# Storing the low parts of the input projection's weights once and reloading them

## The chip, the cores and the metric

The kernel runs on one core of one Trainium2 chip. The metric is the device time of one execution in microseconds (us). Before the change it was 2847.2 us in the median of 3 runs (2840.0 to 2849.79).

## The reference

One layer over 1024 tokens of width 2048, in float32. The input is normalised (RMSNorm) and projected once to 5968 columns, `z = xn @ w_in`. A part of z feeds RWKV-7, a recurrence with a 64 x 64 state in each of 16 heads, token by token. Another feeds sparse attention: an indexer scores all keys for each query, the best 256 admissible keys are selected, and 16 heads attend to them. Both outputs are gated, concatenated and projected:

```
xn = rms_norm(h, norm_g); z = xn @ w_in
z_rw, g_rw, q_lat, kv_lat, k_idx, w_idx, g_ds = split(z)
o_rw = rwkv7_mixer(z_rw, ...); o_ds = dsa_mixer(q_lat, kv_lat, k_idx, w_idx, ...)
h = h + concat(o_rw * silu(g_rw), o_ds * silu(g_ds)) @ w_out
h = h + (p @ ple_w) * sigmoid(h @ ple_gate_w)
out = rms_norm(h, final_g)
```

## The kernel before

Large matrix products are computed in a fast reduced-precision format with correction: both operands are split into a high part (rounded to that format) and a low part (the rest), and three products are summed, high by high, high by low and low by high.

The tokens are handled in two halves of 512 (`hf` 0 and 1), one after the other. The activations of a half (`xh`, `xl`, 16 tiles of 128 channels each) stay on chip. The weights do not: for each half, each of 46 column tiles of `w_z` (128 columns) is streamed as 4 pieces of 128 x 512 numbers (256 KB), 184 pieces in all, and one narrower tile `w_z80` (80 columns) as 4 more. A piece is prepared in `w_piece` (lines 507 to 515): SyncE (SP) issues a load into a buffer `wr` (4 buffers), ScalarE (ACT) rounds it into `wh` (5 buffers), and GpSimd (POOL) subtracts, `wl = wr - wh` (5 buffers). TensorE (PE) then runs 12 matmuls of 128 x 512 on it in `gemm_part`: four channel tiles, three products each. So the same piece is loaded, rounded and subtracted once for each half.

In the same stretch the recurrence runs as 32 steps (`sub`): 8 units of two heads, in two halves, in two quarters of 256 tokens each. A step has a preparation, `chunk_setup`, a long dependent sequence over PE, VectorE (DVE), ACT and POOL (normalising keys, decays, the products `ARb`, `BRb`, `KB`, a triangular inverse by five doublings, `Qf`), and a serial part over 4 chunks of 64 tokens, `chunk_serial`, which runs beside the next step's preparation. A step needs the projections r, k, v and gate of its unit (`zunit`). Projections that no step waits for are the latents of the attention (`dsa_lat`), its gates (`gds`, eight tiles for each half), and the first part of the output projection (`wout_rw`).

The order on each engine is not the order of the program text. `Sched` records all instructions of a stage, a planner (`plan`) simulates the engines with prices and levels, and `emit` writes the instructions out in the planned order; each engine then executes its own list in that order. Chain instructions have level 0, the splitting of weights `LSPLIT` = 1, the projections' matmuls `LG` = 3, the rest `LF` = 4; a lower number goes first. PE takes the fills in short runs between the chain's matmuls. The planner counts a DVE instruction that uses two on-chip operands and a POOL instruction as excluding each other. SP issues every DMA, in its planned order.

When the last step is done the buffers of the recurrence are given up (`nc.emit(RP)`, line 1015), and the second stage begins in their room: index scores of all queries (level `LX` = 2), then the key selection, a bitwise search in which DVE and ACT count, with the rest of the output projection's first part as filler on PE. Attention, the rest of the output projection and the gated second projection follow; these use `w_piece` too, with other weights.

`kept` (lines 911 to 924) already does for the output projection's first part what the change does for the input projection: in the first half it stores `wh` and `wl` in DRAM, in the second it loads both.

Of the kernel before, what the change touches and what calls it, by code (L numbers as in the profile page):

```python
# [10 lines left out]
F32 = mybir.dt.float32  # L11
# [17 lines left out]
LB, LA, LC, LEVAC, LSPLIT, LX, LG, LF, LSQ = 0, 0, 1, 1, 1, 2, 3, 4, 4  # L29
# [356 lines left out]
def hybrid_kernel(ctx, tc, cst, msk, bkt, prm, xt, pt_, w_z, w_z80, w_lora, w_uq, w_iq, w_uk, w_uv, w_o, w_pg,  # L386
                  w_pl, rel_bias, out):
    ctx.enter_context(tc.manual_schedule())
    nc = Sched(tc.nc)
    dram = ctx.enter_context(tc.tile_pool(name="dram", bufs=1, space=DRAM))  # L390
    dt = lambda n, shape: dram.tile(shape, F32, name=n)
# [2 lines left out]
    kid = [dt(f"ki{h}", [64, TH]) for h in range(2)]  # L394
    gdd, h1d = ([[dt(f"{n}{j}_{h}", [128, TH]) for h in range(2)] for j in range(m)] for n, m in (("gd", 8), ("h1", 16)))
    bsk, vbd = dt("bsk", [16, 128, 384]), dt("vb", [16, 384])
    parts = {}

    def pool(stack, keep=None, **kw):
        p_ = Pool(nc, stack.enter_context(tc.tile_pool(**kw)), kw["bufs"])  # L400
# [106 lines left out]
    def w_piece(src, kn, n):  # L507
        wr = wp.tile([128, 4, 128], F32, name="wr", tag="wr", bufs=W_[0])
        nc.sync.dma_start(wr[:, :kn, :n], src.rearrange("p (k n) -> p k n", k=kn))
        with nc.level(LSPLIT):  # L510
            wh = wp.tile([128, 4, 128], F32R, name="wh", tag="wh", bufs=W_[1])
            nc.scalar.activation(wh[:, :kn, :n], wr[:, :kn, :n], AF.Copy)
            wl = wp.tile([128, 4, 128], F32R, name="wl", tag="wl", bufs=W_[1])
            nc.gpsimd.tensor_tensor(wl[:, :kn, :n], wr[:, :kn, :n], wh[:, :kn, :n], op=OP.subtract)
        return wh, wl

    def gemm_part(pz, src, n, k0, kn, nk, xh, xl, w=None):
        wh, wl = w or w_piece(src, kn, n)
        for k in range(kn):
            kk = k0 + k  # L520
            for j, (a, b) in enumerate(((wh, xh), (wh, xl), (wl, xh))):
                nc.tensor.matmul(pz[:n], a[:, k, :n], b(kk), start=(kk == 0 and j == 0),
                                 stop=(kk == nk - 1 and j == 2), skip_group_check=True)
# [16 lines left out]
    def zgroup(tiles, before=lambda g, piece: None):  # L540
        pzs = [pz_tile() for _ in tiles]
        for g in range(4):
            early = []
            before(g, lambda: early.append(w_piece(w_z[tiles[len(early)], g], 4, 128)))
            for j, (pz, i) in enumerate(zip(pzs, tiles)):
                gemm_part(pz, w_z[i, g], 128, g * 4, 4, 16, xh_, xl_, early[j] if early else None)
        return pzs
# [363 lines left out]
    def kept(n, g):  # L911

        if (n, g) in parts:
            pair = []
            for d, nm in zip(parts[n, g], ("wh", "wl")):
                t = wp.tile([128, 4, 128], F32R, name=nm, tag=nm, bufs=W_[1])
                nc.sync.dma_start(t.bitcast(F32), d)
                pair.append(t)
            return pair
        pair = w_piece(w_o[n, g], 4, 128)  # L920
        parts[n, g] = [dt(f"wo{n}_{g}{a}", [128, 4, 128]) for a in "hl"]
        for d, t in zip(parts[n, g], pair):
            nc.sync.dma_start(d, t.bitcast(F32))
        return pair
# [605 lines left out]
```

## Time and profile before

| | |
|---|---|
| time, median of 3 runs | 2847.2 us |
| the profiled execution's own time | 2844.57 us |
| its span, first to last instruction | 2842.8 us |
| mean granted TensorE clock | 0.976 |
| weight pieces split on POOL, all stages | 624 |

PE is the tensor engine's matmuls and PEld its weight loads; the ends of matmuls are modelled, and overlapping ones are counted once in busy times. Since every instruction is issued through one helper, all carry the line number 382; instructions are told apart by the names of the tiles that they write and read, as in `wl<-wr,wh`. Second half means hf = 1, which begins at about 745 us; the first stage with the recurrence ends at about 1600 us.

### The profile page before, as it was taken

What the parts mean: (1) busy time and instruction counts of PE and PEld (TensorE: products, weight loads), DVE (VectorE), ACT (ScalarE), POOL (GpSimd) and SP (SyncE); (2) the same over time, 40 slices, a digit from 0 to 9 for tenths busy, and PEclk for the clock granted to TensorE, in tenths of its full rate; (3) what the DMA queues carried; (4) which work ended last, traced back from release to release, by engine and by line L of the source; (5) the groups of instructions that cost most, each with busy time, mean ns of one, the idle gap of its engine ahead of it and who ended that gap; (6) DMA issues with size and microseconds to landing.
All of it is one profiled execution on the core that took longest, in us unless ns stands there. A gap on an engine that the chain in (4) does not pass through costs nothing. (4 is left out here: it accounts for less than half of the span.)

```text
span 2842.8 us, 46633 instructions
## 1 busy us (share of the span) xinstructions
PE 2701.8 (95%) x16482; PEld 2157.9 (76%) x16482; DVE 1644.8 (58%) x3709; ACT 1482.0 (52%) x3265; POOL 1336.5 (47%) x1371
## 2 busy tenths in 40 slices
PE   7999999999999999999999999948999999999996
PEld 5777778778778778777877788826776788878885
DVE  6457667546764566667665478987666641135312
ACT  5445555535654355555555466895767533343332
POOL 5545445555455545545555421023334455656654
PEclk9999999999999999999999999968999999999998
DMA  4232222232332222222227844511223343355332
GB/s 159 82 116 70 68 71 75 75 89 71 99 100 84 89 68 68 71 69 70 79 82 240 310 146 137 175 36 39 73 65 90 102 138 97 97 157 174 103 99 92
DMA packets 172586, 293.36 MB, mean 103 GB/s; under 512 B 23440, under 2 KB 44992, under 8 KB 172352
## 3 DMA queue, kind: packets, MB, share of 16 engines
q1 hardware_dynamic: 172352, 290.38, 32.9%
q8 instruction: 130, 2.13, 0.3%
q14 instruction: 104, 0.85, 0.1%
HBM read 232.87 MB, written 52.19 MB: 100 GB/s over the span
## 5 line engine op out<-in xcount | busy, mean ns | idle before, releaser
L382 POOL TENSOR_TENSOR wl<-wr,wh 128x512 fp32r<-128x512 f32 (+1 forms) x624 | 812.8, 1306 | 773.5 <-ACT wh L382 720.4
L382 ACT ACTIVATE wh<-wr 128x512 fp32r<-128x512 f32 (+1 forms) x624 | 384.1, 617 | 731.7 <-PE pz L382 536.1
L382 PE MATMUL pz<-xh,wh 128*128 128x512 f32 (+1 forms) x1504 | 609.5, 407 | 11.5 <-ACT wh L382 7.6
L382 PE MATMUL pz<-xh,wl 128*128 128x512 f32 (+1 forms) x1504 | 610.2, 408 | 2.3 <-POOL wl L382 2.1
L382 PE MATMUL pz<-xl,wh 128*128 128x512 f32 (+1 forms) x1504 | 611.1, 408 | 0.0
L382 PEld LDWEIGHTS pz<-xh,wh 128*128 128x128 f32 (+1 forms) x1504 | 285.6, 190 | 62.5 <-ACT wh L382 9.4
L382 PEld LDWEIGHTS pz<-xh,wl 128*128 128x128 f32 (+1 forms) x1504 | 285.1, 190 | 51.4 <-POOL wl L382 5.5
L382 PEld LDWEIGHTS pz<-xl,wh 128*128 128x128 f32 (+1 forms) x1504 | 285.8, 190 | 45.9 <-DVE xl L382 0.3
L382 DVE SCALAR_TENSOR_TENSOR tg<-tg,pg 128x512 f32<-128x512 f32 x32 | 22.0, 687 | 314.3 <-ACT tg L382 303.1
L382 DVE CAST_PREDICATED QX<-MS,pq 128x512 f16<-128x512 uint8 x160 | 110.3, 689 | 158.7 <-PE pq L382 157.6
L382 PE MATMUL pz<-hh,wh 128*128 128x512 f32 x512 | 199.3, 389 | 0.0
L382 PE MATMUL pz<-hh,wl 128*128 128x512 f32 x512 | 199.3, 389 | 0.0
L382 PE MATMUL pz<-hl,wh 128*128 128x512 f32 x512 | 199.2, 389 | 0.0
L382 POOL TENSOR_TENSOR mb<-mk,bt 128x256 f32<-128x256 f32 (+1 forms) x128 | 89.2, 702 | 153.6 <-DVE mx L382 126.3
L382 ACT ACTIVATE Ztb<-pzt 64x256 f16<-64x256 f32 x320 | 120.6, 377 | 61.3 <-PE pzt L382 55.9
L382 ACT ACTIVATE lgt<-lgt,nm 128x128 f32<-128x128 f32 (+7 forms) x128 | 98.8, 772 | 55.0 <-DVE nm L382 54.2
L382 PE MATMUL ptt<-C,lgt 128*128 128x128 f32 x576 | 99.7, 289 | 23.8 <-ACT lgt L382 22.4
L382 ACT ACTIVATE Sw<-UV,Wx 64x64 f32<-64x64 f32 x240 | 82.2, 342 | 58.9 <-DVE UV L382 55.5
L382 PEld LDWEIGHTS pz<-hh,wh 128*128 128x128 f32 x512 | 96.1, 188 | 20.0
L382 PEld LDWEIGHTS pz<-hl,wh 128*128 128x128 f32 x512 | 96.1, 188 | 20.0
L382 PEld LDWEIGHTS pz<-hh,wl 128*128 128x128 f32 x512 | 96.1, 188 | 19.7
L382 PE MATMUL po<-PT,V 128*64 128x128 f32 x1152 | 87.6, 287 | 18.7 <-ACT PT L382 18.2
(331 smaller groups left out, 6008.3 us busy)
## 6 DMA issues: line engine op xcount, KB each, us to landing
wr<-in_w_z_dram SPq DMA_DIRECT2D x368, 256.0 KB, 2.6
wr<-in_w_pg_dram SPq DMA_DIRECT2D x128, 256.0 KB, 2.6
wr<-in_w_o_dram SPq DMA_DIRECT2D x88, 256.0 KB, 2.9
h<-h SPq DMA_DIRECT2D x60, 256.0 KB, 3.2
h<-in_xt_dram SPq DMA_DIRECT2D x32, 256.0 KB, 3.7
out_dram<-h SPq DMA_DIRECT2D x32, 256.0 KB, 2.3
gd<-gd SPq DMA_DIRECT2D x16, 256.0 KB, 2.3
mix<-m SPq DMA_DIRECT2D x32, 128.0 KB, 1.7
```

Of the source, the lines that this page charges most:

```text
L382: getattr(self.real[o.eng], o.name)(*o.args, **o.kw)
```

## The change

The first time that a piece of `w_z` or `w_z80` is prepared, its low part is also stored in a new DRAM tile, at level `LF`. When the same piece is asked for again (found by tensor name and offset), the high part is made as before, from a new load of the weights, and the low part is loaded from DRAM in place of the subtraction, at the level of the splitting. Nothing else is edited; the planner makes new orders for all engines from the new list of instructions.

```diff
-    parts = {}
+    parts, lows, KEEP = {}, {}, (w_z.tensor.name, w_z80.tensor.name)
...
             wl = wp.tile([128, 4, 128], F32R, name="wl", tag="wl", bufs=W_[1])
+            key = src.tensor.name, src.offset
+            if key in lows:
+                nc.sync.dma_start(wl[:, :kn, :n].bitcast(F32), lows[key])
+                return wh, wl
             nc.gpsimd.tensor_tensor(wl[:, :kn, :n], wr[:, :kn, :n], wh[:, :kn, :n], op=OP.subtract)
+        if src.tensor.name in KEEP:
+            lows[key] = dt(f"low{len(lows)}", [128, kn, n])
+            with nc.level(LF):
+                nc.sync.dma_start(lows[key], wl[:, :kn, :n].bitcast(F32))
         return wh, wl
```

## Rows read from the trace of the kernel before

**Rows 1.** Page, busy time, share of the span and instructions of each engine

```profile
PE 2701.8 (95%) x16482; PEld 2157.9 (76%) x16482; DVE 1644.8 (58%) x3709; ACT 1482.0 (52%) x3265; POOL 1336.5 (47%) x1371
```

**Rows 2.** Chain of waits: start us, us, what; one of 15 such

```profile
2623.75 10.88 PE pz L382 x48
```

**Rows 3.** Busy time by stage: us, busy (instructions), PEclk, DMA share, GB/s

```profile
945.00:1390.00 445.00, 444.15 (x3118) 354.99 (x3117) 291.94 (x559) 234.55 (x610) 227.03 (x238) 1.00 0.24 70
...
1600.00:1780.00 180.00, 177.50 (x806) 145.74 (x805) 131.55 (x158) 107.42 (x158) 39.09 (x31) 0.99 0.52 178
1780.00:1850.00 70.00, 67.25 (x375) 58.50 (x374) 67.63 (x263) 59.93 (x108) 6.00 (x6) 1.00 0.54 174
1850.00:1930.00 80.00, 36.75 (x156) 23.99 (x155) 68.57 (x305) 73.92 (x146) 17.63 (x20) 0.62 0.11 29
```

**Rows 4.** Tile hr, 940 to 1530 us: count, ns min/median/max, first and last start

```profile
L382 POOL TENSOR_TENSOR hr<-hs,nh x15: 1001/1006/1318, 945.4 to 1523.6; 128x4 f32<-128x4 f32 x15
```

**Rows 5.** Tile wl, matmuls on PE, 945 to 1512 us

```profile
L382 PE MATMUL pz<-xh,wl x558: 387/393/586, 945.0 to 1511.6; 128*128 128x512 f32 x186
```

**Rows 6.** Tile gd on DVE, 900 to 1600 us

```profile
L382 DVE SCALAR_TENSOR_TENSOR gd<-gd,zd x8: 673/693/1553, 1401.3 to 1515.0; 128x512 f32<-128x512 f32 x8
```

**Rows 7.** Waits of PEld, 745 to 1512 us: total us, times, longest

```profile
PEld pz L382 <- POOL wl L382: 0.4, 2, 0.2
```

**Rows 8.** Groups on POOL, 945 to 1512 us: count, busy us, mean ns, idle before

```profile
L382 POOL TENSOR_TENSOR wl<-wr,wh 128x512 fp32r<-128x512 f32 x140 | 184.6, 1319 | 196.6 <-ACT wh L382 181.0 <-PE pz L382 5.0 <-PE pv L382 4.1
L382 POOL TENSOR_TENSOR BRb<-r,Wx 64x256 f32<-64x256 f32 x28 | 22.3, 796 | 4.4 <-ACT Wx L382 3.4
```

**Rows 9.** Groups on DVE, 945 to 1512 us

```profile
L382 DVE TENSOR_TENSOR ARb<-kkn,Wx 64x256 f32<-64x256 f32 x28 | 24.6, 878 | 1.6 <-ACT Wx L382 1.1
L382 DVE SCALAR_TENSOR_TENSOR KB<-q,iW 64x256 f32<-64x256 f32 x28 | 21.5, 768 | 0.3
L382 DVE TENSOR_TENSOR KB<-kp,iW 64x256 f32<-64x256 f32 x28 | 20.4, 730 | 0.2
...
L382 DVE TENSOR_TENSOR kp<-tha,k 128x256 f32<-128x256 f32 x14 | 11.7, 836 | 0.4
...
L382 DVE COPY hx<-hr 128x256 f32<-128x256 f32 x14 | 8.8, 626 | 2.2 <-POOL hr L382 2.2
```

**Rows 10.** Tiles on DVE, 945 to 1512 us: ns min/median/max, first and last

```profile
L382 DVE TENSOR_TENSOR ARb<-kkn,Wx x28: 417/823/1423, 949.3 to 1487.0; 64x256 f32<-64x256 f32 x28
...
L382 DVE SCALAR_TENSOR_TENSOR KB<-q,iW x28: 406/424/1519, 953.0 to 1488.7; 64x256 f32<-64x256 f32 x28
L382 DVE TENSOR_TENSOR KB<-kp,iW x28: 406/424/1521, 956.4 to 1491.2; 64x256 f32<-64x256 f32 x28
...
L382 DVE TENSOR_TENSOR kp<-tha,k x14: 424/427/1430, 953.9 to 1489.1; 128x256 f32<-128x256 f32 x14
...
L382 DVE COPY hx<-hr x14: 279/678/1371, 947.1 to 1481.5; 128x256 f32<-128x256 f32 x14
```

**Rows 11.** Timeline of POOL, DVE and PE in one step: start, us, instruction

```profile
1326.74 1.58 POOL L382 TENSOR_TENSOR wl<-wr,wh 128x512 fp32r<-128x512 f32 x1 [0.29 <-ACT wh L382]
1329.43 1.40 POOL L382 TENSOR_TENSOR wl<-wr,wh 128x512 fp32r<-128x512 f32 x1 [1.11 <-ACT wh L382]
1330.80 0.73 POOL L382 TENSOR_TENSOR rk<-r,kp 128x256 f32<-128x256 f32 x1
...
1328.84 0.84 DVE L382 TENSOR_TENSOR KB<-kp,iW 64x256 f32<-64x256 f32 x2
...
1332.79 1.05 PE L382 MATMUL pA<-ARb,KB 128*128 128x128 f32 x8
```

**Rows 12.** Busy time by stage, the second ten microseconds of the kernel

```profile
10.00:20.00 10.00, 10.00 (x38) 8.06 (x37) 10.00 (x9) 9.02 (x16) 7.35 (x11) 1.00 1.00 346
```

**Rows 13.** DMA issues: count, KB each, median us to landing

```profile
wr<-in_w_z_dram SPq DMA_DIRECT2D x368, 256.0 KB, 2.6
...
wl<-wo_0l SPq DMA_DIRECT2D x16, 256.0 KB, 3.7
```

## The prediction

> **What bounds the kernel now.** I read the page's busy times first. TensorE (PE) is busy 95% of the span, GpSimd (POOL) 47% [rows 1], so the obvious verdict is that relieving POOL is worth nothing. The chain of waits agrees at the end of the kernel: 48 matmuls take 10.88 us, one each 0.2267 us with nothing between them [rows 2]. A weight piece is 12 such matmuls, 2.72 us of PE.
>
> But a full PE is only a bound if nothing better could be put in its place, so I went on to the table by stage. From 945 to 1390 us PE is busy 444 of 445 us; from 1600 to 1930 us it is idle 2.5 + 2.75 + 43.25 = 48.5 us, most of it in the key selection (1850 to 1930 us), where VectorE (DVE) is busy 68.6 and ScalarE (ACT) 73.9 of 80 us and the granted clock falls to 0.62 [rows 3]. PE has filler (weight pieces and output tiles) in the first part, and has run out of it in the last. The key selection comes behind the index scores, and these can start only when the recurrent chain of `chunk_setup` has ended, because their buffers take the room of its pools. So what counts is when the chain ends. Filler displaced by a faster chain is not lost: it goes into those 48.5 us.
>
> Is the chain bound by latency or by PE? Its marker is the `hr` instruction, one in each of the 32 steps: the last 15 lie between 945.4 and 1523.6 us [rows 4], so 14 intervals of 41.3 us. From 945 to 1512 us PE makes 558 matmuls on low parts, that is 139.5 pieces [rows 5], 379 us at 2.72 us; the other 188 us are 13.7 steps of chain work, 13.7 us each. One head unit (two steps) must have 16 pieces and twice the chain work: 43.5 + 27.4 = 70.9 us, 35.5 us a step. The measured 41.3 us is 5.8 us above that floor. The surplus goes into projecting ahead: the eight `gds` tiles, the filler of lowest priority, are evacuated only from 1401 us on [rows 6], with `hr` still coming up to 1523.6 us [rows 4]. So latency sets the step.
>
> **The change, part by part.**
>
> *Removed: 184 subtractions on POOL in the second half.* PE hardly waits for them itself: in the second half the weight loads waited 0.4 us for `wl` in all [rows 7]. That term I put at nothing. The gain, if there is one, is in what these subtractions do to others. From 945 to 1512 us 140 of them take 184.6 us, 1.32 us each [rows 8], a third of POOL's time. DVE instructions of the chain that read two SBUF operands show two durations: `KB` 0.41 us at best and 0.42 in the median, but up to 1.52 us [rows 10]. I take each group's busy time [rows 9] less count times its shortest [rows 10]: `hx` 8.8 - 14 x 0.279 = 4.9, `ARb` 24.6 - 28 x 0.417 = 12.9, `KB` from q 21.5 - 11.4 = 10.1, `kp` 11.7 - 5.9 = 5.8, `KB` from kp 20.4 - 11.4 = 9.0; together 42.7 us in 14 steps. Who causes it? POOL's `BRb` (22.3 us, rows 8) lies in the same place and stays. If all of it is charged first, 20.4 us are left for `wl`; shared by POOL time, 184.6 / 206.9 of 42.7, it is 38 us. I take the middle, 29 us.
>
> The Trainium skill (SBUF — State Buffer, "Who interferes with whom") says that a DVE instruction with two SBUF inputs and a GpSimd instruction that reads SBUF exclude each other, and whichever issued first blocks the other fully. The trace agrees with the form of it: the excess of the longest `KB`, 1.1 us, is most of one subtraction. By that rule every one of the 42.7 us is somebody's lock, and with the pieces spread at random `wl` would have the 38 us rather than the 29: a sum 9 us better.
>
> *Removed with it: waiting in POOL's own queue.* In the step at 1326 us one subtraction starts at 1326.74, the next at 1329.43, and `rk` starts only behind it at 1330.80; PE has the product on `rk` ahead of `pA`, which starts at 1332.79, though the last `KB` was done at 1329.68 [rows 11]. POOL is in a subtraction a third of the time, so a POOL instruction of the chain finds one in its way with that chance and waits half of 1.32 us: 0.2 us. Four on the path (`hr`, `BRb`, `rk`, `IX`) in 14 steps make 12 us at most, 0 at least; I take 6.
>
> So the chain would end 29 + 6 = 35 us earlier (from 20 to 50). PE's order is written out in advance by the kernel's own planner, which counts POOL against DVE too; it will set fewer fillers between the chain's matmuls. Since the 48.5 us of idle PE behind it exceed 35 us, all of it reaches the end; what is late next is filler, beyond a gain of 48.5 us.
>
> *Added: 184 stores in the first half*, 256 KB each. They wait for `wl`, and SyncE (SP) queues behind them; but the next load of `wr` into that buffer already waits for the same subtraction. POOL waits for nothing new while the store takes less than the four pieces that PE still has ahead (10.9 us). Only the start is tight: from 10 to 20 us DMA is at 1.00 of its time, at 346 GB/s [rows 12]. Twelve stores there are 12 x 0.262 MB / 346 GB/s = 9.1 us if all delay a load, 0 if they fill the gaps. I take 3 us.
>
> The Trainium skill (SBUF — State Buffer, "SBUF: two separate sides") says that engine ports and DMA ports are disjoint, so that a DMA cannot be slowed by a compute instruction or the reverse; by it the 94 MB of extra traffic cost the engines nothing, and the sum loses only what the transfers take from each other. No row here tests that.
>
> *Added: 184 loads in the second half.* A piece now lands twice, `wr` in 2.6 us and the low part in about 3.7 us, which the existing reload of `wo` shows [rows 13]. With five buffers it may be issued four pieces (10.9 us) ahead. DMA's share from 945 to 1390 us is 0.24 [rows 3]; the pieces' first landing is nearly all of its 70 GB/s (140 x 0.262 MB in 567 us are 65), so the share would about double. Hidden, at 0; if the cover is gone PE waits for each piece (rival 3). ACT's conversion of the high part stays. SP's queue has the load where it had the wait for POOL.
>
> **Sum.** 2844.6 us of the profiled execution (span 2842.8) - 35 + 3 = 2812.6. The median of the runs shown, 2847.2, is 2.6 us above that execution, so I forecast **2815 us**. Its own ends: -50 + 0 gives 2797, -20 + 9 gives 2836.
>
> **Rivals.**
> 1. *The chain gains nothing* (chance 0.14). For it: PE shows 444 of 445 us busy, and its written order may be re-planned with as much filler between the chain's steps; DVE instructions that get shorter then only wait longer. Against it: 5.8 us a step above PE's floor. Removed waits 0.4 us, start +3: about 2850 us, within 0.3% (8.5 us, about what a measurement of this kernel can tell from no change) of before.
> 2. *The chain gains more than POOL's share*, because a looser plan also shortens its waits on PE (0.16). Down to the floor it would be 14 x 5.8 = 81 us, but idle PE behind it has only 48.5: 2799 us or a little less.
> 3. *Slower: the low parts land too late* (0.14). SP issues in order. If a load of a low part stands in its queue for a buffer that PE has not yet released, everything behind it, `wr` included, waits too. It decides where landing and queueing together exceed 10.9 us, so a queue wait beyond 7.2 us. The half switch and the latent tiles, where PE runs pieces back to back, are its place. At 0.1 us for each of 184 pieces and the 9 us of the start it is 2847 + 27 = 2874 us with no gain from the chain. Against it: DMA at 0.24.
>
> That the change doesn't do what it says (a key that never matches) would leave only the stores, and fall under rival 1.
>
> **Numbers.** Forecast 0.56, rivals 0.14, 0.16, 0.14. Faster by over 0.3%: 0.56 + 0.16 = 0.72; within: 0.14; slower: 0.14. Range 2795 to 2852: it holds the forecast, most of rival 1 and the upper part of rival 2, and leaves out most of rival 3.
>
> **What would show it.** In the table by stage of the changed kernel, POOL at about a fifth of the second half; the 14 intervals of `hr` at about 38.8 us; `KB` and `kp` nearer their shortest; the key selection ending some 32 us earlier, and PE's idle time there shorter by as much. Wrong: intervals still at 41 us (rival 1), weight loads waiting for the low parts' transfers (rival 3), or an index stage that starts earlier and then takes longer, so that the gain is given back.

## The result: 2799 us, and the profile after

The changed kernel took 2799.2 us (median of 4 runs, 2793.5 to 2801.9), the kernel before 2847.4 us beside it: a ratio of 0.9832, with a 95% interval of 0.9808 to 0.9857, so 48 us faster. The forecast was 2815 us; 2799 us is the number that stood for rival 2 (the chain gains more, down to PE's floor). It lies in the stated range, 2795 to 2852, near its lower end.

The page of the changed kernel, first the busy times (the same columns as [rows 1]), then the traffic and three of its DMA issues (as [rows 13]):

```profile
PE 2693.5 (96%) x16482; PEld 2150.1 (77%) x16482; DVE 1584.2 (57%) x3709; ACT 1489.8 (53%) x3265; POOL 1109.4 (40%) x1183
...
DMA packets 229805, 391.19 MB, mean 140 GB/s; under 512 B 33552, under 2 KB 55104, under 8 KB 229568
...
wr<-in_w_z_dram SPq DMA_DIRECT2D x368, 256.0 KB, 2.9
low<-wl SPq DMA_DIRECT2D x184, 256.0 KB, 3.2
wl<-low SPq DMA_DIRECT2D x184, 256.0 KB, 2.6
```

PE has the same 16482 instructions. POOL has 188 fewer and 227 us less work, and 184 stores and 184 loads of 256 KB are new, with four of 160 KB each way for the narrow tile: 97.8 MB more traffic than the 293.4 MB of before. The profiled span is 2799.8 us, 43.0 us shorter. Since PE is at work nearly all the time, the 43.0 us can be split by PE's own time: idle time went from 2842.8 - 2701.8 = 141.0 to 2799.8 - 2693.5 = 106.3 us, which is 34.7 us less, and the same matmuls took 8.3 us less.

The marker of the recurrent chain in the changed kernel answers to [rows 4]:

```profile
L382 POOL TENSOR_TENSOR hr<-hs,nh x15: 1007/1008/1377, 955.0 to 1456.1; 128x4 f32<-128x4 f32 x15
```

Fourteen intervals are 501.1 us, 35.8 us each; before they were 41.3. The first of the 15 starts 9.6 us later than before, the last 67.5 us earlier. The floor that the prediction worked out was 35.5 us.

Where the steps became shorter is seen in PE's matmuls on low parts, of which each weight piece has four. Between the first and the last of the 15 markers the kernel before has

```profile
L382 PE MATMUL pz<-xh,wl x559: 387/393/586, 945.0 to 1512.4; 128*128 128x512 f32 x187
```

and the changed kernel

```profile
L382 PE MATMUL pz<-xh,wl x451: 387/393/776, 956.1 to 1455.8; 128*128 128x512 f32 x151
```

That is 27 pieces less between the steps, 73 us of PE at 2.72 us each, of the 77 us by which the 14 intervals became shorter. What is left is 32.2 such matmuls a step; the prediction's floor, eight pieces a step, has 32.

The table by stage of the changed kernel, the same windows and columns as [rows 3]:

```profile
945.00:1390.00 445.00, 442.57 (x3256) 351.38 (x3255) 281.79 (x630) 251.19 (x659) 98.18 (x147) 1.00 0.40 126
1600.00:1780.00 180.00, 175.48 (x788) 143.07 (x787) 155.48 (x358) 131.41 (x213) 52.51 (x36) 1.00 0.69 232
1780.00:1850.00 70.00, 67.97 (x314) 55.34 (x313) 62.49 (x230) 60.73 (x108) 13.24 (x7) 1.00 0.71 232
1850.00:1930.00 80.00, 70.35 (x500) 56.45 (x499) 54.05 (x181) 48.82 (x100) 37.09 (x40) 0.94 0.21 58
```

PE is as full as before in the recurrence (442.6 of 445 us), but with more done: DVE and ACT issue 71 and 49 instructions more in it. Of 1600 to 1930 us PE is now idle 4.5 + 2.0 + 9.7 = 16.2 us where it was 48.5. That is 32.3 of the 34.7 us. Of the rest, PE is idle 7.0 us more in the first 750 us, 1.4 more from there to 1600 us, and 10.8 less after 1930 us. The granted clock of the last row went from 0.62 to 0.94.

What PE waited for from 1600 to 1950 us (total us, times, longest), first the kernel before:

```profile
PE ptt L382 <- ACT lgt L382: 21.8, 5, 12.5
PE plg L382 <- DVE mx L382: 21.3, 9, 5.5
```

and the changed kernel:

```profile
...
PE plg L382 <- DVE mx L382: 2.8, 4, 1.6
...
PE ptt L382 <- ACT lgt L382: 0.2, 1, 0.2
```

`plg` and `ptt` are the first matmuls of attention; their softmax (`mx` on DVE, `lgt` on ACT) had to stand behind the key selection on both engines. The selection's counting on ACT, from the kernel before:

```profile
L382 ACT ACTIVATE js<-mk,th x93: 920/1041/1153, 1786.4 to 1918.9; 128x1024 f16<-128x1024 f32 x31, 128x896 f16<-128x896 f32 x31, 128x768 f16<-128x768 f32 x31
```

and from the changed one:

```profile
L382 ACT ACTIVATE js<-mk,th x93: 921/1043/1152, 1714.5 to 1838.0; 128x1024 f16<-128x1024 f32 x31, 128x896 f16<-128x896 f32 x31, 128x768 f16<-128x768 f32 x31
```

It ends 81 us earlier. PE's filler, the first part of the output projection, no longer ends ahead of it but beside it. These are its matmuls in the changed kernel from 1780 to 1900 us:

```profile
L382 PE MATMUL pz<-ml,wh x81: 388/389/397, 1779.9 to 1835.6; 128*128 128x512 f32 x81
```

Before, the last one was at 1818.9 us. So the selection ends 81 us earlier, PE's idle time could take up less than that, and the kernel ends 43 us earlier in the profile. What is late now should be filler; this is tested below.

### The profile page after: what moved, and what is told of

Same layout as the page of the kernel before. It is cut to its first block, busy times and chain, and to the rows that moved or that the text cites. A ratio compares the mean times of both kernels' runs of the same rounds, so it can differ in the third digit from the quotient of the medians.

```text
span 2799.8 us, 47033 instructions
## 1 busy us (share of the span) xinstructions
PE 2693.5 (96%) x16482; PEld 2150.1 (77%) x16482; DVE 1584.2 (57%) x3709; ACT 1489.8 (53%) x3265; POOL 1109.4 (40%) x1183
## 5 line engine op out<-in xcount | busy, mean ns | idle before, releaser
L382 POOL TENSOR_TENSOR wl<-wr,wh 128x512 fp32r<-128x512 f32 (+2 forms) x436 | 574.6, 1321 | 561.0 <-ACT wh L382 528.7
L382 DVE SCALAR_TENSOR_TENSOR mk<-rl,WI,mk 128x384 f32<-128x384 f32 (+2 forms) x90 | 101.1, 1165 | 9.2 <-ACT rl L382 8.8
L382 PE MATMUL pz<-mh,wh 128*128 128x512 f32 x256 | 99.5, 393 | 5.5 <-DMA wh<-wo_0h 3.2
```

Of the source, the lines that this page charges most:

```text
L382: getattr(self.real[o.eng], o.name)(*o.args, **o.kw)
```

## The experiments

Those named together ran on the same chip. Each ratio is to the kernel before on that chip.

### Stores alone, and loads alone

`e1_stores_only` leaves the subtractions of the second half in place:

```diff
-            if key in lows:
-                nc.sync.dma_start(wl[:, :kn, :n].bitcast(F32), lows[key])
-                return wh, wl
-        if src.tensor.name in KEEP:
+        if src.tensor.name in KEEP and key not in lows:
```

> Stores of the first half alone; the second half subtracts as before the change. Theory (the stores cost the first half what the trace after shows, hr of step 17 at 955.0 instead of 945.4 us, and nothing else changes): about 2857 us, intervals of hr in the second half still 41 us. Rival (the stores cost nothing, the delay is only the planner's other order): 2845 to 2850 us.

Measured: 2855.2 us against 2847.2, ratio 1.0033 (1.0020 to 1.0046). The stores cost 8 us. Its `hr` intervals are 41.3 us, from 959.2 to 1537.8 us: the recurrence of the second half is untouched and starts 14 us late.

`e2_loads_only` stores one piece of each width and lets all 184 loads read that one, so that the low parts of the second half are those of another piece:

```diff
-                nc.sync.dma_start(wl[:, :kn, :n].bitcast(F32), lows[key])
+                nc.sync.dma_start(wl[:, :kn, :n].bitcast(F32), lows[n])
...
+            if n not in lows:
+                lows[n] = dt(f"low{n}", [128, kn, n])
+                with nc.level(LF):
+                    nc.sync.dma_start(lows[n], wl[:, :kn, :n].bitcast(F32))
```

> Loads of the second half alone: one piece of each width is stored, and all 184 loads read that one, so the low parts of the second half have the wrong numbers; the traffic of the loads is the same, 182 stores are left out. Theory (stores cost some 10 us of PE time in the first half, which reach the end): 2789 us, step 17 at 945 us, intervals of hr at 36 us. Rival (what bounds the end is something behind the chain, so an earlier chain gives nothing more): 2799 us.

Measured: 2792.6 us, ratio 0.9811 (0.9794 to 0.9828); `hr` from 945.4 to 1445.7 us, 35.7 us a step. The start of the 15 steps is that of before to the tenth, so the 9.6 us that the changed kernel loses there are the stores'. At the end of the kernel about 6 us of it are seen, within the width of the two intervals.

Where do the stores cost? In the first 750 us PE is idle 23.6 us before and 30.6 after. ACT's waits there for a fresh weight piece, in the kernel before (total us, times, longest):

```profile
ACT wh L382 <- DMA wr<-in_w_z_dram: 24.7, 11, 8.1
```

and in the changed kernel:

```profile
ACT wh L382 <- DMA wr<-in_w_z_dram: 43.0, 22, 6.9
```

The fresh weight piece comes late, twice as often. Over kernels with different stores (some of them are told further down) this wait and PE's idle time mostly go together:

| first 750 us | ACT's wait for `wr` | PE idle | DMA share |
|---|---|---|---|
| before | 24.7 | 23.6 | 0.29 |
| e2_loads_only (2 stores) | 25.4 | 25.3 | 0.29 |
| v4_units_early_store (112 stores) | 24.7 | 27.6 | 0.39 |
| e8_store_without_hold (172 stores) | 33.1 | 26.4 | 0.47 |
| v5_rkv_only (84 stores) | 37.0 | 27.8 | 0.38 |
| v1_units_only (112 stores) | 38.7 | 27.9 | 0.40 |
| e1_stores_only | 40.3 | 31.7 | 0.49 |
| the changed kernel | 43.0 | 30.6 | 0.49 |
| e3_old_order | 59.5 | 35.6 | 0.46 |

The last row has the longest wait without the highest DMA share, so traffic alone does not set it. `v4_units_early_store` has more idle time than before without a longer wait, so late weights are not the only cost either. A second one shows in the changed kernel, in what POOL waited for in its first 750 us; before the change there is no such row:

```profile
POOL wl L382 <- DMA low<-wl: 12.4, 5, 3.4
```

POOL waits there for the buffer of a low part that a store still holds.

### The relief without the new order, and the new order without the relief

The prediction took the gain from shorter DVE instructions, yet the written order changes too. Two kernels take them apart, on the chip of the two above. `e3_old_order` lets the planner see a subtraction as before and swaps it for the load when the instructions are written out, so PE, DVE and ACT keep the order of the kernel before:

```diff
+            if o.swap:
+                self.real["sync"].dma_start(*o.swap)
+            else:
+                getattr(self.real[o.eng], o.name)(*o.args, **o.kw)
+            if o.also:
+                self.real["sync"].dma_start(*o.also)
...
+                if key in lows:
+                    nc.ops[-1].swap = wl[:, :kn, :n].bitcast(F32), lows[key]
+                else:
+                    lows[key] = dt(f"low{len(lows)}", [128, kn, n])
+                    nc.ops[-1].also = lows[key], wl[:, :kn, :n].bitcast(F32)
```

> Old order, new work: the planner plans the list of before, with the subtractions on POOL; when the instructions are written out, each subtraction of the second half is replaced by the load on SP, and a store is put behind each of the first half. PE, ACT and DVE have exactly the order of before. Theory (the gain came through the order that the planner writes, which has fewer fillers between the chain's matmuls): intervals stay at 41 us, 2847 to 2857 us. Rival (POOL's relief works by itself, whatever the order): intervals below 39 us and 2800 to 2825 us.

Measured: 2868.5 us, ratio 1.0073 (1.0056 to 1.0090), slower than before. Tile `hr` in it, and its groups on DVE from 945 to 1450 us:

```profile
L386 POOL TENSOR_TENSOR hr<-hs,nh x15: 1007/1008/1318, 970.3 to 1547.9; 128x4 f32<-128x4 f32 x15
```

```profile
L386 DVE TENSOR_TENSOR ARb<-kkn,Wx 64x256 f32<-64x256 f32 x24 | 15.4, 643 | 1.5 <-ACT Wx L386 1.1
L386 DVE TENSOR_TENSOR KB<-kp,iW 64x256 f32<-64x256 f32 x24 | 14.0, 583 | 0.2
L386 DVE SCALAR_TENSOR_TENSOR KB<-q,iW 64x256 f32<-64x256 f32 x24 | 11.6, 485 | 0.3
...
L386 DVE COPY hx<-hr 128x256 f32<-128x256 f32 x12 | 5.2, 434 | 1.3 <-POOL hr L386 1.3
L386 DVE TENSOR_TENSOR kp<-tha,k 128x256 f32<-128x256 f32 x12 | 5.1, 426 | 0.4
```

The relief is there: by the prediction's own count (busy time less count times the shortest of [rows 10]) the excess is 13.4 us in 12 steps, 1.1 us a step where it was 42.7 / 14 = 3.0. The intervals are 41.3 us all the same. PE's order holds as much filler between the chain's matmuls as before (559 on low parts between the first and last marker, in both kernels), PE is busy 574.6 of these 577.6 us, and the DVE time that is saved becomes waiting. So the steps of the kernel before were held by PE's written order, not by the speed of DVE and POOL. The intervals came as expected; the time, 2847 to 2857 us, did not. What the run lost, it lost ahead of these 15 steps: its marker comes 25 us late already in the first of them (the section on the stores' cost below).

`e4_new_plan_old_work` does the reverse. The subtractions of the second half stay, but the planner prices them at 0.01 and takes no lock for them; nothing is stored or reloaded:

```diff
+            key = src.tensor.name, src.offset
+            if key in seen:
+                nc.ops[-1].lock, nc.ops[-1].cost = False, 0.01
+            elif src.tensor.name in KEEP:
+                seen.add(key)
```

> New plan, old work: no stores and no loads, all subtractions done on POOL, but the planner is told that those of the second half take no time and exclude no DVE instruction. Theory (order and relief are both needed): the order offers 36 us a step, but 1.32 us of POOL for each piece are still there, so intervals of 38 to 40 us and 2815 to 2835 us. Rival A (order alone does it): 36 us and about 2790 us. Rival B (POOL's time is the real bound): 41 us or more, 2847 us or slower.

Measured: 2843.0 us, ratio 0.9987 (0.9978 to 0.9997). Its `hr`, a row of its table by stage, and what PE waited for from 945 to 1500 us:

```profile
L382 POOL TENSOR_TENSOR hr<-hs,nh x15: 1007/1007/1121, 955.4 to 1494.5; 128x4 f32<-128x4 f32 x15
```

```profile
945.00:1390.00 445.00, 414.58 (x3002) 324.34 (x3001) 311.20 (x586) 232.19 (x608) 214.15 (x231) 1.00 0.21 62
```

```profile
PE pch L382 <- DVE UV L382: 14.9, 13, 1.6
PE pres L382 <- DVE QX L382: 6.4, 13, 0.8
PE pch L382 <- DVE rh L382: 4.3, 5, 0.9
PE pb L382 <- DVE hx L382: 3.6, 6, 0.6
PE pb L382 <- POOL rk L382: 2.3, 2, 1.7
```

The order is not quite that of the changed kernel, since its list of instructions has no loads or stores, but it holds as little filler: 448 matmuls on low parts between the first and last marker. The chain does gain, 41.3 to 38.5 us a step, but PE now stands 30.4 us idle in the window in which it was idle 0.85, behind DVE and POOL, which are as slow as before (the excess of the five DVE groups, counted as above, is 3.3 us a step). In exchange PE is idle 12.5 us from 1600 to 1930 us where it was 48.5 (PE busy 317.54 of 330 us there). Idle time has moved from one stage to the other and the kernel ends 4 us earlier. The intervals were as expected; the time, 2815 to 2835 us, was missed for that reason: the earlier end of the chain was counted as gain, PE's new waits were not. Neither half brings much alone; together, and without the stores, they bring 55 us (`e2_loads_only`).

### Is PE's filler what is late?

The last 5 of the 16 output tiles of the second half's first part, 27.2 us of matmuls, are left out, with the loads of their weights and their additions, of the kernel before (`e5_before_less_filler`) and of the changed one (`e6_after_less_filler`), so their part of the result is missing:

```diff
-            pz = pz_tile()
-            for g in range(2):
+            pz = None if hf == 1 and n > 10 else pz_tile()
+            for g in range(2 if pz is not None else 0):
...
+            if pz is None:
+                nc.sync.dma_start(h_, xt[n * 128:n * 128 + 128, hf * TH:hf * TH + TH])
+                store(h1d[n][hf], h_)
+                continue
```

> The kernel before, with filler taken away: the last 5 of the 16 output tiles of the second half's first part of the output projection are left out (their matmuls, weights and additions; the residual alone is passed on), 5 x 24 x 0.2267 = 27.2 us of PE. Theory (before the change PE runs out of filler in the key selection, so filler is free): 2840 to 2847 us. Rival (PE is the bound throughout): 2820 us.

> The changed kernel with the same filler taken away. Theory (after the change filler on PE is what is late behind the chain, which is why 67 us of earlier chain gave only 43 to 48): 2799 - 27 = 2772 us, or a little more once the chain is the bound again, and the difference to the run before of this list is far larger than to its own parent. Rival (something else behind the chain, DMA in the output tiles or the key selection, took the rest): 2790 to 2799 us.

Measured: the kernel before without them 2848.2 us against 2844.9 (ratio 1.0011, 1.0002 to 1.0020), so they were free there (without them it is, if anything, 3 us slower). The changed kernel without them takes 2781.8 us (0.9775, 0.9753 to 0.9796), 17 us below the 2799 of the changed kernel, which was not run beside it, or 16 us by the two ratios. The last stage of the first one:

```profile
1850.00:1930.00 80.00, 18.34 (x60) 12.28 (x62) 65.65 (x288) 76.75 (x143) 9.92 (x10) 0.56 0.07 16
```

and of the second:

```profile
1850.00:1930.00 80.00, 67.61 (x457) 48.20 (x457) 65.59 (x249) 50.07 (x110) 34.98 (x46) 0.91 0.20 52
```

Before the change PE's idle time from 1600 to 1930 us grows from 48.5 to 77.2 us, 43.3 to 61.7 of it in this last stage, and the end stays. After it the work left out comes off the end, but 16 or 17 of 27 us only, where 2772 us had been expected: PE's idle time from 1600 to 1930 us grows from 16.2 to 23.5 us, and the key selection starts its last count at 1849.0 us, 11.0 us later than in the changed kernel. So filler was late behind the chain, but not all that was; how the other 10 us come about in the newly planned order isn't shown.

### Fewer pieces

If the gain lies in the chain's steps, the pieces prepared between them should carry all of it. `v1_units_only` keeps 112 of the 184 pieces (the r, k, v and gate tiles of units 1 to 7), `v5_rkv_only` 84 of them (without the gates), `v4_units_early_store` is the first with the store at the level of the splitting, ahead of other transfers.

```diff
-        if src.tensor.name in KEEP:
+        if src.tensor.name == KEEP[0] and src.offset // TILE in UNITS:
...
```

> Only the 112 pieces of units 1 to 7, which PE runs beside the recurrence's steps in the second half, are stored and reloaded; the other 72 (the first unit, the latents, the gates) are subtracted again. Theory (the gain is made in steps 17 to 31, the cost by the stores of the first half): intervals of 36 to 37 us as in the changed kernel while these pieces last, a smaller delay of the first half (about 6 us instead of 10), 2795 us. Rival (the gates' subtractions from about 1390 us on, and the latents', matter too): 2800 to 2815 us.

> The same 112 pieces, with the stores at the level of the splitting instead of the lowest. Theory (a store that waits in SP's queue keeps its buffer from the next subtraction): delay of the first half smaller still, 2790 to 2795 us. Rival (an early store stands before the loads of the next pieces and PE waits for these): 2800 us or more.

> The changed kernel once more, on the same chip as the two that follow, for their comparison: 2799 us, 0.983 of before.

> The 112 pieces of units 1 to 7 once more, beside the changed kernel on one chip. Theory (fewer stores cost the first half less, the chain's gain stays): 5 to 8 us below the changed kernel, 0.981 of before. Rival (the difference between the chips of the two earlier runs): equal to it within 3 us.

> Only the r, k and v tiles of units 1 to 7, 84 pieces. Theory (the chain's 77 us are more than the PE idle behind it can take up, so some of them can be given away for fewer stores): intervals of hr near 37 us, a delay of the first half of 3 us, time equal to that of the 112 pieces or some us below, 2789 to 2794 us. Rival (each subtraction left in the steps costs its share of the gain): intervals of 38 us or more and 2800 us or more.

| kernel | us | ratio | `hr`, us a step |
|---|---|---|---|
| v1_units_only | 2792.4 | 0.9806 (0.9792 to 0.9821) | 36.2 |
| v4_units_early_store | 2799.4 | 0.9827 (0.9811 to 0.9843) | 36.2 |
| after_again (the changed kernel) | 2798.8 | 0.9829 (0.9816 to 0.9843) | 35.7 |
| v1_again | 2792.1 | 0.9813 (0.9797 to 0.9830) | 36.2 |
| v5_rkv_only | 2794.2 | 0.9814 (0.9800 to 0.9827) | 36.2 |

The first two ran on one chip, the other three on another. 84 of 184 pieces bring all the gain, and 112 are some 5 to 7 us below the changed kernel in both of its runs; the intervals still overlap, so that difference is likely and not settled. The marker of step 17, 9.6 us late in the changed kernel, is 3.8 us late with 112 stores and 2.0 us with 84. Storing earlier doesn't help: 2799.4 us is 7 us above the same pieces stored late, on the same chip, with intervals that just overlap, and step 17 is 9.4 us late again. The time is what its rival said, but the rival's reason isn't shown: ACT waits for `wr` no longer than before the change, and POOL 2.0 us for a buffer that a store holds. What an early store costs stays open.

### Why a store costs what it does

In `e3_old_order` the way to the second half took longest. From `hr` of step 0 to that of step 17 it is 970.3 - 70.5 = 899.8 us, before 945.4 - 64.6 = 880.8 us. A store there waits for `wl` in SP's queue and keeps the `wl` buffer until it has landed. `e8_store_without_hold` has the order and the subtractions of before and 172 stores of 256 KB in the same places, but out of a constant tile, so that nothing is waited for or held (and nothing is reloaded):

```diff
+                if READY and key not in lows:
+                    lows[key] = dt(f"low{len(lows)}", [128, kn, n])
+                    nc.ops[-1].also = lows[key], C[:, :kn * n].rearrange("p (k n) -> p k n", k=kn)
...
```

> Order of before on PE, ACT, DVE and POOL, all subtractions done, no reloads; behind each subtraction of the first half but the first 12 SP issues a store of 256 KB as in the run with the old order, but out of the constants, so that it waits for no subtraction and holds no buffer of a low part. That run took 899.8 us from hr of step 0 to that of step 17, the kernel before 880.8. Theory (the delay comes from SP waiting at the store and from the held buffer): below 886 us. Rival (the extra traffic and SP's issue time alone delay the loads): 895 us or more.

Measured: 2850.0 us, ratio 1.0008 (0.9998 to 1.0018), and 953.7 - 64.9 = 888.8 us between the two steps: 8 of the 19 us. Neither expectation holds. The other 11 us are not all for waiting and holding, because `e3_old_order` also reloads low parts from the start of the second half on. Steps 0 to 15 are the first half; their markers in the kernel before, in `e3_old_order` and in `e8_store_without_hold`:

```profile
L382 POOL TENSOR_TENSOR hr<-hs,nh x16: 1006/1007/1458, 64.6 to 775.4; 128x4 f32<-128x4 f32 x16
L386 POOL TENSOR_TENSOR hr<-hs,nh x16: 1007/1008/1465, 70.5 to 794.2; 128x4 f32<-128x4 f32 x16
L386 POOL TENSOR_TENSOR hr<-hs,nh x16: 1006/1007/1457, 64.9 to 784.0; 128x4 f32<-128x4 f32 x16
```

From step 0 to step 15 it is 710.8, 723.7 and 719.1 us: 8.3 us for traffic and issue, 4.6 us more where the stores wait. From step 15 to step 17 it is 170.0, 176.1 and 169.7 us, and in these 6 us of `e3_old_order` PE waits for reloaded low parts, from 770 to 970 us:

```profile
PE pz L386 <- DMA wl<-low: 4.6, 5, 1.6
```

That is rival 3 in small, at the place that it named, under an order that was planned without the loads; PE of the changed kernel has no such wait. And the first stores, which `e8_store_without_hold` leaves out, are the likely reason why step 0 itself comes 5.9 us late in `e3_old_order`.

The 4.6 us are hardly the held buffer: POOL waits 0.3 us for it in the first 750 us of that run. There a fresh `wr` also lands as fast as before (2.7 us in the median from 60 to 750 us, before 2.6), and ACT waits longest for it; so it is issued late, and the store ahead of it, which waits for `wl` in SP's queue, is the likely reason. In `e8_store_without_hold` it lands in 2.9 us. How much of the 8 us is the traffic in memory and how much SP's time to issue isn't told apart, nor is the share of each in the changed kernel, whose stores lie elsewhere.

## Why the prediction was right in its direction and too small, step by step

- *The range*: 2799 us lies in it, but by the way of rival 2 and not by that of the forecast.
- *What bounds the kernel*: right in that the steps could fall to PE's floor, 35.8 us against 35.5 worked out, and that the displaced filler goes into the idle time of the key selection. "So latency sets the step" was not right of the chip: in the kernel before PE is busy 575.0 of the 578.2 us between the markers, and with shorter DVE instructions under the same order the step stayed at 41.3 us (`e3_old_order`). Latency counted in the planner: told that the subtractions take no time, it sets 448 matmuls on low parts between the markers in place of 559 (`e4_new_plan_old_work`).
- *PE's own waits for `wl` at nothing*: right, and with the change none is listed.
- *Shorter DVE instructions, 29 us*: the size of the relief was right, what follows from it was not. These are the groups of [rows 9] in the changed kernel, 945 to 1450 us:

```profile
L382 DVE TENSOR_TENSOR KB<-kp,iW 64x256 f32<-64x256 f32 x28 | 18.1, 646 | 0.5
L382 DVE TENSOR_TENSOR ARb<-kkn,Wx 64x256 f32<-64x256 f32 x28 | 16.3, 582 | 0.7
...
L382 DVE SCALAR_TENSOR_TENSOR KB<-q,iW 64x256 f32<-64x256 f32 x28 | 11.7, 418 | 0.3
...
L382 DVE COPY hx<-hr 128x256 f32<-128x256 f32 x14 | 6.9, 496 | 2.1 <-POOL hr L382 2.0
...
L382 DVE TENSOR_TENSOR kp<-tha,k 128x256 f32<-128x256 f32 x14 | 6.0, 425 | 0.4
```

  Their excess is 3.0 + 4.6 + 0.3 + 0.1 + 6.7 = 14.7 us, 28 less than the 42.7 of before: the 29 us were there. But the excess is not what the chain gains. In `e3_old_order` it is about as small and the step stays at 41.3 us.
- *Waiting in POOL's own queue, 6 us*: no run shows this term by itself; under the old order it and the one above brought nothing together. In the step of [rows 11] PE did not wait for `rk`, which was done at 1331.53 us: it ran matmuls of weight pieces until it took up the product on `rk` at 1332.36 us.
- *"So the chain would end 29 + 6 = 35 us earlier"*: this is the term that failed. Fourteen steps gained 77 us (5.5 each, not 2.5). The planner had set each step out for a POOL that was held by subtractions; without them it sets less filler between the chain's matmuls, 27 pieces in 14 steps. The prediction named that as a consequence of the gain; it is its carrier: 0 from the relief alone, 2.8 us a step from the order alone, 5.5 from both. The prediction gave this 0.16, as rival 2.
- *The lock* (the Trainium skill, SBUF — State Buffer, "Who interferes with whom"): the measured 28 us are nearer the 29 that POOL's `BRb` was given a share of than the 38 of that reading. With the subtractions gone `KB` from q is at its shortest throughout (407 to 424 ns, before up to 1519), which agrees with the form of the rule. `hx`, counted with the instructions of two operands, is a copy that reads one; its excess fell too, from 4.9 to 3.0 us.
- *All of it reaches the end, since 48.5 us of idle PE exceed it*: with 77 us the cap decided, but it is not a strict one. 32.3 of the 48.5 us were used, 16.2 stay as many short waits. That the idle time fell by the 32 us that were named as a sign is luck, since the chain ended 67.5 us earlier and not 35. Outside the 48.5 us two things were gained that the prediction had no term for. PE is idle 10.8 us less after 1930 us, and the matmuls took 8.3 us less: attention's `ptt`, for one, took 383 ns on average from 1800 to 1960 us before (50 of them) and takes 287 after (128), at a granted clock that is higher [rows 3]; over all 576 the mean went from 289 to 282. Without the stores the gain is above the cap: in the profile of `e2_loads_only` PE's idle time is 43.3 us less and its matmuls 14.3 us less than before.
- *Stores at 3 us*: too small. They cost 8 us (`e1_stores_only`). The place was wrong too: step 0 starts only 1.0 us later (`hr` at 65.6, before 64.6), so the tight start holds little of it; it gathers over the first half, with ACT waiting for late `wr`. "POOL waits for nothing new" was not right: it waited 12.4 us for buffers that stores held. The 94 MB of added traffic were 97.8.
- *Loads at nothing*: right for the changed kernel. The low parts land in 2.4 to 4.3 us, 2.6 in the median, from 945 to 1450 us, the DMA share is 0.40 (about double was said), and rival 3 has no wait to show there. Only under the old order does PE wait for a reloaded low part, 4.6 us (`e3_old_order`).

The two sizes were off in opposite directions: the chain by 42 us too little, of which some 21 reached the end (the 16 us between forecast and result, and the 5 that the stores cost above the forecast).

## What to carry to other kernels

Where an order is planned ahead and written out, ask what the new order makes of a relieved engine: here shortening the work under the old order brought nothing, and the new order over the old work only moved the idle time. A bottleneck engine at 95% says nothing against such a change, if its low-priority work fits into idle time of a later stage; sum that idle time first, as it is roughly the cap (48 us gained of 48.5 here, 55 without the stores). Extra stores are not free just because DMA is half idle: price them by the loads that come later behind them, and make them only for the pieces that lie beside the chain (84 of 184 brought all the gain here).

## What the runs showed of the hardware

- With DMA at 0.49 of its time in the first 750 us, a fresh `wr` still landed later: 3.0 us in the median, before 2.6. Beside this delay on about 190 loads stand 18 us more of ACT's waiting.
- A load can be late without landing late: in `e3_old_order` a fresh `wr` landed in 2.7 us in the median, with stores that wait in the same queue ahead of it, and ACT waited 59.5 us for such pieces where it had waited 24.7.
- TensorE's granted clock from 1850 to 1930 us, a mean over its levels of 1.2 and 2.4 GHz, was 0.62 with PE busy 37 of 80 us, 0.56 with 18 us (`e5_before_less_filler`) and 0.94 with 70 us. With the higher clock attention's matmuls in that stage were shorter, a gain beside the idle time that I had not counted.
